# An encoder layer on one core: two gate products run along with the arrival of x, and two numbers of its planner are changed

## The chip, the core and the metric

The kernel runs on one core of a Trainium2 chip. The metric is the device time of one execution in microseconds (us), taken as the median over runs. Engines are named as in the profile: PE multiplies matrices (PEld loads its weights), DVE and ACT work elementwise, POOL and SP mostly issue transfers (DMA).

## The reference, cut to what matters

One layer over 512 tokens of 1024 channels, all in float32:

```
qa, ka, va, qb, kb, vb = split(x @ w_in)           # then partial rotary on q and k
o_a = windowed attention with sinks (16 query heads, 4 key heads)
o_b = three dilated window attentions (12 heads), merged
g_a, g_b = split(sigmoid(x @ w_gate + b_gate))     # w_gate: 1024 x 2048
y = (g_a * (o_a @ w_br_a) + g_b * (o_b @ w_br_b)) @ w_out
h = layer_norm(alpha * x + y)
out = layer_norm(alpha * h + (silu(h @ w_ff_gate) * (h @ w_ff_up)) @ w_ff_down)
```

## The kernel before, in words

**Numbers.** Each float32 operand is split into a high part `h` (a rounded copy) and a low part `l` (the rest). A product over 128 rows of the contraction is then three matmuls of 128 x 512: h by h, h by l, l by h. They stand on L513, L514 and L515 in `feat_k`, and one such call is called a product step here; a whole product over 1024 channels has eight (k = 0 to 7). A weight unit is 128 x 1024 values (512 KB), loaded in two halves of 256 KB. `half_unit` does it in the ordinary case: a transfer (L371, on SP's queue), a copy to `h` (L363, on ACT), a subtraction to `l` (L389, on DVE).

**The start.** The first units of k, q and v (`psk`, `psq`, `psv`, three PSUM banks) are multiplied while x arrives: x comes in eight blocks of 256 KB (xs[0] to xs[7], L481), each split by an L363 copy and an L486 subtraction, and PE takes k, q and v of block 0, then of block 1, and so on. The weights of these three are cut into pieces (`half_unit_by`, `CUTS`, subtractions on L422), and the table `FIRST` gives each piece its place among the transfers. Beside this, DVE and ACT form sums of the x blocks for later (`x_forms`, L534 and L560). Then an order written as a string (`ORDER`) goes on: `g2` two gate products (16 products of 128 columns make all gates), `VA` the second half of v and its transposes (L895), `q1` the next queries, `A0` the first attention group (scores on L860 and L861), and so on. `P:` products and all feed-forward products use seven half-size products for eight, for which some weights are sums of two blocks. Such a sum is fetched by `load_sum`: a plain transfer from SP, then one from POOL that adds while it writes (L377), an accumulating transfer.

**The branches.** After the attentions, `branch_a` and `branch_b` multiply their outputs by w_br_a and w_br_b; `gated` (L1387, on DVE) multiplies the gate with the bank and so makes it free, L1409 adds the two branches, L1355 (ACT) and L1363 (DVE) split the sum, and w_out is multiplied token-major (L1453 to L1455). At that time the first feed-forward weights are fetched already.

**The feed-forward** runs over 22 units of 128 columns (`quad`, matmuls on L1663 to L1665), with the down product in three chunks (`Chunk.step`, L1874 to L1876) between them and the rest token-major at the end. `silus` lists the activations of the units.

**What sets the order.** All operations are handed to a planner (`Program.run`), which goes through a clock of its own (`now`), starts on each engine the ready operation of the lowest priority number for which there are buffers, and issues it at once: the order in which it starts operations is the order of the instructions on each engine. It reckons an accumulating transfer's end thus (`moves` is the time of its bytes):

```
moved = max(moved, end + 0.3) + (1.0 if now < SLOW else 0.92) * o.moves
o.done = moved + (0.87 if e == ACT else 3.2 if now < SLOW else 2.2)
```

`SLOW` (300) is also the time after which plain transfers from SP are reckoned with an end 0.87 after their bytes, and not 2.4. Buffers are counted by class: `whl` (split weights), `ws` (weights as they land), `gen` (all else); `pr.spare` (12) is how many `gen` buffers are kept back from operations that are not first in line. `POOL 0.0` operations change such limits in the course of the plan.

Of the kernel before, what the change touches and what calls it, by code (L numbers as in the profile page):

```python
# [9 lines left out]
F32 = mybir.dt.float32  # L10
# [5 lines left out]
P = 128  # L16
S = 512
# [14 lines left out]
U_KA = 0  # L32
# [26 lines left out]
SPARE_OUT = 4  # L59
BANKS = dict(dense=3, s=2, tb=2, o=1, d=8)  # L60
UNITS = 2
SLOW = 300
SPIN = 4

CUTS = ((0, 128), (128, 256), (256, 512))
# [1 line left out]
         ("k", 1): (-996.9,), ("q", 1): (-996.7,), ("v", 1): (-996.6,),  # L67
         "x": (-999, -998.75, -997.5, -996.95, -996.8, -996.5, -996.4, -996.3)}
X_PACE = {1: None}
N_WS, N_WHL, N_ATT, N_GEN = 6, 12, 16, 60  # L70


# [5 lines left out]


ORDER = """  # L80
g2 VA q1 A0 q2 q3 g X k1 q4 A1 P:q5,g P:q6,q7 R A2 P:g,g A3 g g2 L Q00 K00 R Q01 K01 R V12 Q02 K02 R V0 B0 Q10 K10 R Q11 K11 R B1 Q12 K12 R B2 B3 g7
"""
FORMS = -60.0
PACK = -60.0
# [39 lines left out]
class Program:  # L124
# [67 lines left out]
    def run(self):  # L192
# [26 lines left out]
        while n_left:  # L219
# [11 lines left out]
            while progress:  # L231
                progress = False
                for e in engines:
# [27 lines left out]
                    if e == SP:  # L261
                        end = now + (0.62 if 14 < now < SLOW else 0.47)
                        moved = max(moved, now + 0.9) + (1.5 if now < 9.5 else 1.0 if now < SLOW else 0.92) * cost
                        o.done = moved + (2.4 if 14 < now < SLOW else 0.87)
                    elif o.moves:
                        end = now + cost
                        moved = max(moved, end + 0.3) + (1.0 if now < SLOW else 0.92) * o.moves
                        o.done = moved + (0.87 if e == ACT else 3.2 if now < SLOW else 2.2)
                    else:
                        end = now + cost  # L270
                        o.done = end
# [50 lines left out]
def hybrid_layer(ctx: ExitStack, tc: tile.TileContext, wpack, xT, xtok, sink, bgate,  # L322
# [6 lines left out]

    N_SLOT, HP = 85, S // 2  # L330
    pr = Program({"slot": N_SLOT, "bank": 8, **BANKS,
                  "ws": N_WSA, "whl": N_WHLA, "att": N_ATT, "gen": N_GEN,
                  "unit": UNITS, "st": 4, "x4": 4, "wf": N_WF})
    op = pr.op
    mm = nc.tensor.matmul
# [130 lines left out]

    first = {}
    for j in range(2):
        for w, u in (("k", U_KA), ("q", U_QA), ("v", U_VA)):
            first[w, j] = half_unit_by(u, j, ((0, S),) if j else CUTS, FIRST[w, j])  # L470
    got, xs = {}, []
    for j in range(KD):
        st, ap = slot(F32, "xs"), FIRST["x"][j]
# [751 lines left out]
        op([(SP, 0.73)], lambda e: nc.sync.dma_start(d.t, t.t), reads=[t], writes=[d], prio=EV)  # L1225
        away[f] = d

    def gate(f, put=False):
        ps = bank("dense")
        feat_x(ps, unit(U_GATE + f))  # L1230
        t = slot()
        gz[f] = t
        op([(ACT, act(S, True, 1))], lambda e: nc.scalar.activation(
            halves(t.t), back(ps.t), AF.Tanh, bias=bg.t[:, f:f + 1], scale=0.5),
           reads=[ps, bg], writes=[t], prio=EV)
        if put:
            d = Buf("dram", None, lambda: dram.tile([P, S], F32, name=name("gz")))
            op([(SP, 0.73)], lambda e: nc.sync.dma_start(d.t, t.t), reads=[t], writes=[d], prio=EV)
            away[f] = d

    def dense_q(u, nt, kv_half):
        ps = bank("dense")
# [6 lines left out]
        return k_post(ps, nt) if nt else k_pairs(ps)  # L1249

    psk, psq, psv = bank("dense"), bank("dense"), bank("dense")
    for k in range(KD):
        for w, ps in (("k", psk), ("q", psq), ("v", psv)):
            for c in (0, S // 2) if (w, k) == ("k", 0) else (None,):
                if c is None:
                    feat_k(ps, [first[w, 0], first[w, 1]], k, XM, xtok_of, split=w == "k")
                else:
                    op_ = feat_k(ps, [first[w, 0], first[w, 1]], k, XM, lambda k, c=c: [(xh4[0], 0, c), (xl4[0], 0, c)],
                                 n0=c, n1=c + S // 2, begins=c == 0, split=True)
                    if c == 0:  # L1260
                        fill(op_)
    ka = k_near(psk, 4)
    qa = q_near(psq, 4, (0, 0))
    load(mB, maskb, prio=0)
    env = {"gate": 0, "turn": [], "qs": {}, "ks": {}}

    def units_of(w):
        i = int(w[1:] or 0)
# [15 lines left out]
    def step(w):  # L1284
# [27 lines left out]
        elif w == "k1":  # L1312
            ka.extend(dense_k(U_KA + 1, 4))
        elif w[0] == "A":
            g = int(w[1])
            for b in range(NR):
                unit_a(g, b, qa[4 * g:4 * g + 4], ka[g], env["va"])
        elif w[0] in "gG":
            for _ in range(int(w[1:] or 1)):
                gate((env["gate"] + 8) % 16, w[0] == "G")  # L1320
                env["gate"] += 1
        elif w[0] in "QK":
            pair, g = int(w[1]), int(w[2])
            u, f = units_of(w)
            env["turn"].append((in_sbuf(u), f))
        elif w == "V0":
            env["v0"] = turned_values(U_V0, 8, 1)
        elif w == "V12":
            env["v1"], env["v2"] = token_values(U_VB)
        elif w[0] == "B":  # L1330
            hs = int(w[1])
            unit_b(hs, [env["qs"][hs // 2, g][hs % 2] for g in range(3)],
                   [env["ks"][hs // 2, g][hs % 2] for g in range(3)], env["v0"], env["v1"], env["v2"])
            if hs in ROOMS:
                op([(POOL, 0.0)], lambda e: pr.limits.update(ROOMS[hs]), after=list(exps))
# [575 lines left out]
            out[t, :, j * S + c0:j * S + c1], xt[t, j].t[:, c0:c1]), reads=[tok])  # L1911

    op([(POOL, 0.0)], lambda e: pr.limits.update(whl=4 * (N_LAST + 2)), after=[silus[-2]])
    n0 = 2 * N_PAIR * N_CHUNK
    tok_major(NFF - n0, N_LAST, lambda k: su[n0 + k], U_DOWN + n0, lg2, lb2, store, True, 1.0,
              lambda t: [chunks[c].step(n) for c, n in STEPS.get(("block", t), ())], (2, 3))
# [101 lines left out]
```

## Time and profile before

| | |
|---|---|
| median of 3 runs | 740.82 us (740.76 to 741.11) |
| the profiled execution | 739.78 us, of which the span of instructions is 737.9 us |
| busy | PE 723.1, PEld 662.9, DVE 661.0, ACT 460.7, POOL 118.8 us |
| granted PE clock | 0.998 |
| moved by DMA | 126.62 MB, on average 172 GB/s |

The profile is one execution, followed by the hardware. A row of its timeline is: start, duration, engine, line, operation, output and inputs, shapes, count, and in brackets the idle time before it with what ended that. Matmuls overlap in it: each is shown for 0.28 to 0.48 us, but one of 128 x 512 starts every 0.216 us when nothing holds PE. How long PE waits is therefore read from the starts.

### The profile page before, as it was taken

To read this page: it belongs to the slowest core of one execution; us is meant where nothing else is said; L and a number is where in the kernel's file an instruction comes from. 1 tells how busy PE (TensorE), PEld (TensorE's weight loads), DVE (VectorE), ACT (ScalarE), POOL (GpSimd) and SP (SyncE) were. 2 spreads that over 40 slices of the span, in tenths; PEclk is the share of its full clock that TensorE was granted. 3 is DMA by queue.
4 is the path that set the end of the run, shared out by engine and by line. 5 is a ranking of instruction groups with operands and counts; after the bars stand their busy time and mean duration, and the time that the engine had idled before them with its cause. 6 is when DMAs were issued, how large, how long until landed. Compare 5 with 4: busy or idle time off the path is not lost.

```text
span 737.9 us, 13854 instructions
## 1 busy us (share of the span) xinstructions
PE 723.1 (98%) x4587; PEld 662.9 (90%) x4587; DVE 661.0 (90%) x1445; ACT 460.7 (62%) x1041; POOL 118.8 (16%) x279
## 2 busy tenths in 40 slices
PE   8999999999999999999989999999999999999996
PEld 5888999888888888898878999999999999999985
DVE  6998999899888897789977999799999999899987
ACT  5765797776676676565643557656666556666721
POOL 0021001100000460360011012111102211212100
PEclk9999999999999999999999999999999999999999
DMA  8876666126724367745874289866888878978502
GB/s 261 268 178 164 159 197 170 41 84 160 202 66 122 121 182 194 197 138 169 267 191 115 74 251 229 191 176 153 203 247 200 223 183 234 250 198 176 118 29 85
DMA packets 73718, 126.62 MB, mean 172 GB/s; under 512 B 9904, under 2 KB 14128, under 8 KB 73648
## 3 DMA queue, kind: packets, MB, share of 16 engines
q1 hardware_dynamic: 62640, 105.96, 47.0%
q0 software_dynamic: 10736, 19.67, 16.5%
q8 instruction: 36, 0.59, 0.3%
q14 instruction: 34, 0.28, 0.1%
q10 hardware_dynamic: 272, 0.13, 0.1%
HBM read 106.32 MB, written 2.88 MB: 148 GB/s over the span
## 4 chain that ended last, share of the span: by engine, by line
PE 90%; DMA 5%; DVE 2%; SPq 1%; ACT 1%; issue 1%; DVEq 0%; ACTq 0%
PE ps L513 9%; PE ps L514 9%; PE ps L515 9%; PE ps L1663 9%; PE ps L1665 9%; PE ps L1664 9%; PE ps L1874 4%; PE ps L1876 4%; PE ps L1875 4%; PE ps L963 3%; PE ps L1453 3%; PE ps L1455 3%; PE ps L1454 3%; DMA sl<-wpack 2%; PE ps L861 1%; PE ps L860 1%
## 5 line engine op out<-in xcount | busy, mean ns | idle before, releaser
L363 ACT ACTIVATE sl<-sl 128x512 fp32r<-128x512 f32 (+3 forms) x401 | 220.9, 585 | 40.5 <-DVE sl L534 19.5
L534 DVE TENSOR_TENSOR sl<-sl,sl 128x512 fp32r<-128x512 f32 (+3 forms) x333 | 192.2, 615 | 8.0 <-DMA sl<-wpack 3.8
L363 ACT ACTIVATE sl<-ps 128x256 f32<-128x256 f32 (+6 forms) x210 | 89.9, 446 | 96.9 <-PE ps L1665 59.7
L513 PE MATMUL ps<-x,sl 128*128 128x512 f32 (+1 forms) x321 | 123.3, 384 | 0.9 <-ACT x L363 0.8
L515 PE MATMUL ps<-x,sl 128*128 128x512 f32 (+1 forms) x321 | 121.6, 379 | 0.4 <-DVE sl L422 0.4
L514 PE MATMUL ps<-x,sl 128*128 128x512 f32 (+1 forms) x289 | 109.8, 380 | 0.9 <-DVE x L486 0.8
L1663 PE MATMUL ps<-sl,sl 128*128 128x256 f32 x352 | 96.9, 275 | 0.6 <-ACT sl L363 0.6
L1664 PE MATMUL ps<-sl,sl 128*128 128x256 f32 x352 | 96.8, 275 | 0.0
L1665 PE MATMUL ps<-sl,sl 128*128 128x256 f32 x352 | 96.8, 275 | 0.0
L377 POOL DMA_DIRECT2D sl<-wpack x50 | 44.1, 886 | 314.0 <-DVE sl L534 95.2
L389 DVE TENSOR_TENSOR sl<-sl,sl 128x512 fp32r<-128x512 f32 x118 | 79.1, 684 | 3.5 <-ACT sl L363 3.1
L1663 PE MATMUL ps<-x,sl 128*128 128x256 f32 x264 | 72.6, 275 | 0.0
L1664 PE MATMUL ps<-x,sl 128*128 128x256 f32 x264 | 72.6, 275 | 0.0
L1665 PE MATMUL ps<-x,sl 128*128 128x256 f32 x264 | 72.6, 275 | 0.0
L515 PEld LDWEIGHTS ps<-x,sl 128*128 128x128 f32 x321 | 60.7, 189 | 9.4 <-DVE sl L422 0.9
L513 PEld LDWEIGHTS ps<-x,sl 128*128 128x128 f32 x321 | 60.8, 189 | 8.8 <-ACT x L363 1.5
L1663 PEld LDWEIGHTS ps<-sl,sl 128*128 128x128 f32 x352 | 67.6, 192 | 0.8 <-ACT sl L363 0.7
L1664 PEld LDWEIGHTS ps<-sl,sl 128*128 128x128 f32 x352 | 67.6, 192 | 0.1
L1665 PEld LDWEIGHTS ps<-sl,sl 128*128 128x128 f32 x352 | 67.6, 192 | 0.0
L514 PEld LDWEIGHTS ps<-x,sl 128*128 128x128 f32 x289 | 54.7, 189 | 8.2 <-DVE x L486 2.3
L1016 ACT ACTIVATE sl<-sl,st 128x257 f32<-128x257 f32 (+1 forms) x64 | 35.7, 560 | 26.9 <-DVE st L1012 25.0
L1663 PEld LDWEIGHTS ps<-x,sl 128*128 128x128 f32 x264 | 50.6, 192 | 0.4
(174 smaller groups left out, 1680.4 us busy)
## 6 DMA issues: line engine op xcount, KB each, us to landing
sl<-wpack SPq DMA_DIRECT2D x246, 256.0 KB, 3.9
sl<-sl SPq DMA_DIRECT2D x110, 128.0 KB, 2.4
wf<-wpack SPq DMA_DIRECT2D x51, 256.0 KB, 5.0
sl<-wpack POOLq DMA_DIRECT2D x50, 256.0 KB, 5.7
wf<-wpack POOLq DMA_DIRECT2D x24, 256.0 KB, 6.1
sl<-xtok SPq DMA_DIRECT2D x8, 256.0 KB, 4.0
sl<-sl SPq DMA_DIRECT2D x60, 32.0 KB, 2.0
out<-sl SPq DMA_DIRECT2D x7, 256.0 KB, 2.0
```

The costliest lines, as they stand in the source:

```text
L363: nc.scalar.activation(dst, src, AF.Copy)
L377: op([(POOL, 1.0)], lambda e: nc.gpsimd.dma_start(b.t, src2, accum_op=ALU.add), reads=[b], writes=[b], prio=prio, moves=1.65)
L389: op([(DVE, dve(S))], lambda e: nc.vector.tensor_tensor(l.t, src.t, f32(h.t), op=ALU.subtract), reads=[src, h], writes=[l], prio=prio, abs ...
L513: mm(o, a, x0, start=(k == 0 and begins), stop=False, skip_group_check=split)
L514: mm(o, a, x1, start=False, stop=False, skip_group_check=split)
L515: mm(o, b, x0, start=False, stop=(k == nk - 1), skip_group_check=split)
L534: op([(DVE, dve(w))], lambda e: nc.vector.tensor_tensor(dst(), x(), y(), op=o), reads=reads, writes=writes, prio=prio)
L1016: exps.append(op([(ACT, act(n + 1, extra=2))], lambda e, p=p, h=h: nc.scalar.activation(p.t[:, :n + 1], p.t[:, :n + 1], AF.Exp, bias=st.t[ ...
L1663: mm(o, wh, pairs(bh[k]()), start=(first and k == 0), stop=False, skip_group_check=True)
L1664: mm(o, wh, pairs(bl[k]()), start=False, stop=False, skip_group_check=True)
L1665: mm(o, wl, pairs(bh[k]()), start=False, stop=(k == 3), skip_group_check=True)
L1874: mm(ps.t, x0, pairs(w[0].t), start=(first and m == 0), stop=False, skip_group_check=True)
```

## The change

Three things are done.

1. The first two gate products (`N_ALONG = 2`, gates 8 and 9) move from the string (`g2`) into the start: they are multiplied with each x block just after k, q and v, into two banks of class `s`. Their weights are loaded with the start's (`half_unit_by`, first half in two pieces of 256 columns, `ALONG_CUTS`), at places that `FIRST` gives them: two pieces ahead of the last pieces of k, q and v's first halves, two behind, and the second halves among the later x blocks. The limit of `whl` begins at 24 and goes to 16 when the last of these product steps starts.
2. The planner reckons the end of an accumulating transfer as 6.2 behind its bytes while its clock stands between 330 and 420 (it was 3.2 or 2.2), and `SLOW` goes from 300 to 340.
3. From the third last activation of the feed-forward on, 8 `gen` buffers are kept back instead of 12.

```diff
-SLOW = 300
+SLOW = 340
+N_ALONG, N_WHL0 = 2, 24
+ALONG_CUTS = ((0, 256), (256, 512))
+FIRST.update({(0, 0): (-997.45, -996.97), (0, 1): (-996.65,), (1, 0): (-997.4, -996.96), (1, 1): (-996.45,)})
...
 ORDER = """
-g2 VA q1 A0 q2 q3 g X k1 q4 A1 P:q5,g P:q6,q7 R A2 P:g,g A3 g g2 L Q00 K00 ...
+VA q1 A0 q2 q3 g X k1 q4 A1 P:q5,g P:q6,q7 R A2 P:g,g A3 g g2 L Q00 K00 ...
...
-                        o.done = moved + (0.87 if e == ACT else 3.2 if now < SLOW else 2.2)
+                        o.done = moved + (0.87 if e == ACT else 6.2 if 330 < now < 420 else 3.2 if now < SLOW else 2.2)
...
-                  "ws": N_WSA, "whl": N_WHLA, "att": N_ATT, "gen": N_GEN,
+                  "ws": N_WSA, "whl": N_WHL0, "att": N_ATT, "gen": N_GEN,
...
-        for w, u in (("k", U_KA), ("q", U_QA), ("v", U_VA)):
-            first[w, j] = half_unit_by(u, j, ((0, S),) if j else CUTS, FIRST[w, j])
+        for w, u in (("k", U_KA), ("q", U_QA), ("v", U_VA), *((i, U_GATE + 8 + i) for i in range(N_ALONG))):
+            first[w, j] = half_unit_by(u, j, ((0, S),) if j else ALONG_CUTS if w in range(N_ALONG) else CUTS, FIRST[w, j])
...
-    def gate(f, put=False):
-        ps = bank("dense")
-        feat_x(ps, unit(U_GATE + f))
+    def gate(f, ps=None):
+        if ps is None:
+            ps = bank("dense")
+            feat_x(ps, unit(U_GATE + f))
...
     psk, psq, psv = bank("dense"), bank("dense"), bank("dense")
+    along = [bank("s") for _ in range(N_ALONG)]
     for k in range(KD):
-        for w, ps in (("k", psk), ("q", psq), ("v", psv)):
+        for w, ps in (("k", psk), ("q", psq), ("v", psv), *enumerate(along)):
...
+    op([(POOL, 0.0)], lambda e: pr.limits.update(whl=N_WHLA, ws=N_WSA), after=[pr.ops[-1]])
+    for f in range(N_ALONG):
+        gate(8 + f, ps=along[f])
...
-    env = {"gate": 0, "turn": [], "qs": {}, "ks": {}}
+    env = {"gate": N_ALONG, "turn": [], "qs": {}, "ks": {}}
...
     op([(POOL, 0.0)], lambda e: pr.limits.update(whl=4 * (N_LAST + 2)), after=[silus[-2]])
+    op([(POOL, 0.0)], lambda e: setattr(pr, 'spare', 8), after=[silus[-3]])
```

The matmuls are the same in number and shape before and after; what changes is where they stand. Lines after the change are 3 or 4 higher for the same statement (L513 is L516, L1387 is L1391).

On SP's queue at the start, after the third x block (`sl8`), before: the last pieces of k, q and v (`sl3`, `sl5`, `sl6`), then the fourth x block (`sl17`).

```order
L481 DMA sl8_98<-xT 128x512
L418 DMA sl3_75<-wpack 128x256
L418 DMA sl5_83<-wpack 128x256
L418 DMA sl6_85<-wpack 128x256
L481 DMA sl17_130<-xT 128x512
```

And after, where `sl12` and `sl13` are the two gates' first halves and `sl23` is the fourth x block:

```order
L484 DMA sl8_98<-xT 128x512
L421 DMA sl12_105<-wpack 128x256
L421 DMA sl13_109<-wpack 128x256
L421 DMA sl3_75<-wpack 128x256
L421 DMA sl5_83<-wpack 128x256
L421 DMA sl6_85<-wpack 128x256
L421 DMA sl12_105<-wpack 128x256
L421 DMA sl13_109<-wpack 128x256
L484 DMA sl23_159<-xT 128x512
```

Four pieces of 128 KB stand ahead of the fourth x block that did not, two of them ahead of the last pieces of k, q and v.

On PE at the same time, after block 1 of x, before: block 2 for k, q and v (`ps14`, `ps18`, `ps20`).

```order
L513 MATMUL ps14_112<-x47_94,sl9_100 128x512
L514 MATMUL ps14_112<-x411_103,sl9_100 128x512
L515 MATMUL ps14_112<-x47_94,sl10_101 128x512
L513 MATMUL ps18_134<-x47_94,sl12_109 128x512
L514 MATMUL ps18_134<-x411_103,sl12_109 128x512
L515 MATMUL ps18_134<-x47_94,sl13_110 128x512
```

And after: the two gates (`ps29`, `ps32`) for block 0, and then the same two for block 1.

```order
L516 MATMUL ps29_182<-x47_94,sl21_156 128x512
L517 MATMUL ps29_182<-x411_103,sl21_156 128x512
L518 MATMUL ps29_182<-x47_94,sl22_157 128x512
L516 MATMUL ps32_193<-x47_94,sl25_167 128x512
L517 MATMUL ps32_193<-x411_103,sl25_167 128x512
L518 MATMUL ps32_193<-x47_94,sl26_168 128x512
```

From block 2 on, all five follow each other for each block. What came after the two gate products before, comes directly after block 7 now.

On DVE in the branches, before: behind one L1387 stands the sum `sl1130`, which reads `sl1148`, a buffer that an accumulating transfer fills (L377); the next L1387 is two rows behind it.

```order
L1387 SCALAR_TENSOR_TENSOR sl379_1663<-sl379_1663,ps1176_5057 128x512
L534 TENSOR_TENSOR sl1130_4902<-sl1148_4963,sl1130_4902 128x512
L1409 TENSOR_TENSOR sl965_4166<-sl965_4166,sl379_1663 128x512
L1387 SCALAR_TENSOR_TENSOR sl1166_5024<-sl1166_5024,ps1170_5040 128x512
L1363 SCALAR_TENSOR_TENSOR sl1180_5086<-sl965_4166,sl1179_5085 128x512
```

And after:

```order
L1391 SCALAR_TENSOR_TENSOR sl374_1658<-sl374_1658,ps1176_5063 128x512
L1413 TENSOR_TENSOR sl965_4172<-sl965_4172,sl374_1658 128x512
L1367 SCALAR_TENSOR_TENSOR sl1180_5088<-sl965_4172,sl1179_5087 128x512
L1391 SCALAR_TENSOR_TENSOR sl1166_5030<-sl1166_5030,ps1170_5046 128x512
L1413 TENSOR_TENSOR sl945_4098<-sl945_4098,sl1166_5030 128x512
L537 TENSOR_TENSOR sl1182_5102<-sl1137_4936,sl1181_5101 128x512
L537 TENSOR_TENSOR sl1130_4908<-sl1148_4969,sl1130_4908 128x512
```

The sum that waits for the accumulating transfer has moved from one row behind the first L1387 to six rows behind it, past the second. PE's order of instructions is the same in both kernels from within the attention of mixer B (row 1313 of 4539) to row 4214, and again in the last 148 rows; between row 177 and row 1313, and between row 4214 and row 4391, it differs.

More of the change, by code (lines that the diff above doesn't have):

```diff
@@ L80 @@
 ORDER = """
-g2 VA q1 A0 q2 q3 g X k1 q4 A1 P:q5,g P:q6,q7 R A2 P:g,g A3 g g2 L Q00 K00 R Q01 K01 R V12 Q02 K02 R V0 B0 Q10 K10 R Q11 K11 R B1 Q12 K12 R B2 B3 g7
+VA q1 A0 q2 q3 g X k1 q4 A1 P:q5,g P:q6,q7 R A2 P:g,g A3 g g2 L Q00 K00 R Q01 K01 R V12 Q02 K02 R V0 B0 Q10 K10 R Q11 K11 R B1 Q12 K12 R B2 B3 g7
 """
@@ L1235, in gate @@
            reads=[ps, bg], writes=[t], prio=EV)
[L1236 to L1239, printed above, removed]
     def dense_q(u, nt, kv_half):
@@ L1319, in step @@
             for _ in range(int(w[1:] or 1)):
-                gate((env["gate"] + 8) % 16, w[0] == "G")
+                gate((env["gate"] + 8) % 16)
                 env["gate"] += 1
```

## The prediction

> **What bounds the kernel now.** I read the page's heads, then the stretches, then PE's timeline for every gap between starts.
>
> ```profile
> span 737.9 us, 13854 instructions
> PE 723.1 (98%) x4587; PEld 662.9 (90%) x4587; DVE 661.0 (90%) x1445; ACT 460.7 (62%) x1041; POOL 118.8 (16%) x279
> PE 90%; DMA 5%; DVE 2%; SPq 1%; ACT 1%; issue 1%; DVEq 0%; ACTq 0%
> ...
> core 0: us, PE busy (x) PEld busy (x) DVE busy (x) ACT busy (x) POOL busy (x), PEclk, DMA share, GB/s
> 0.00:10.00 10.00, 7.91 (x31) 4.82 (x32) 4.87 (x16) 4.82 (x12) 0.91 (x5) 1.00 0.69 183
> 10.00:20.00 10.00, 8.74 (x36) 5.92 (x35) 8.68 (x18) 6.99 (x13) 0.00 (x0) 1.00 1.01 342
> 20.00:30.00 10.00, 10.00 (x48) 8.77 (x47) 10.00 (x22) 6.83 (x14) 0.00 (x0) 1.00 0.93 301
> 30.00:45.00 15.00, 14.03 (x69) 12.00 (x68) 14.48 (x28) 11.73 (x22) 2.45 (x7) 1.00 0.82 244
> 45.00:380.00 335.00, 332.74 (x1887) 299.86 (x1884) 295.10 (x747) 223.07 (x537) 58.97 (x204) 1.00 0.56 156
> 380.00:400.00 20.00, 19.71 (x91) 17.15 (x92) 15.53 (x27) 9.39 (x16) 3.48 (x4) 1.00 0.55 136
> 680.00:700.00 20.00, 19.45 (x149) 18.54 (x148) 19.69 (x41) 16.00 (x38) 2.62 (x3) 1.00 0.61 138
> ```
>
> PE is busy for 98% of the span and carries 90% of the chain, at full clock in every stretch. The change takes no matmul away, so it can only win where PE waits: the first 20 us, the waits near 43 and 380 (in 45:380 PE lacks 2.26 of 335, which is the stretch from 377.74 to 380) and one near 688. These are the places, in PE's timeline:
>
> ```profile
> 10.14 0.38 PE L513 MATMUL ps<-x,sl 128*128 128x512 f32 x1
> ...
> 13.19 0.48 PE L514 MATMUL ps<-x,sl 128*128 128x512 f32 x1 [0.24 <-DVE x L486]
> ...
> 16.85 0.48 PE L515 MATMUL ps<-x,sl 128*128 128x512 f32 x1 [0.38 <-DVE sl L422]
> ...
> 18.73 0.48 PE L514 MATMUL ps<-x,sl 128*128 128x512 f32 x1 [0.53 <-DVE x L486]
> ...
> 24.44 0.38 PE L513 MATMUL ps<-x,sl 128*128 128x512 f32 x1
> ...
> 34.80 0.38 PE L513 MATMUL ps<-x,sl 128*128 128x512 f32 x1
> ...
> 43.17 0.55 PE L895 MATMUL ps<-ident,sl 128*128 128x128 f32 x3 [0.97 <-ACT sl L363]
> ...
> 47.23 0.27 PE L860 MATMUL ps<-sl,sl 128*128 128x256 f32 x1
> ...
> 377.36 0.38 PE L1455 MATMUL ps<-sl,sl 128*128 128x512 f32 x1
> 380.29 0.48 PE L513 MATMUL ps<-sl,sl 128*128 128x512 f32 x1 [2.55 <-DVE sl L1387]
> ...
> 687.83 0.28 PE L1665 MATMUL ps<-sl,sl 128*128 128x256 f32 x1
> 688.65 0.38 PE L1663 MATMUL ps<-sl,sl 128*128 128x256 f32 x1 [0.55 <-ACT sl L363]
> ```
>
> 10.14 is the first step of x block 2, 24.44 the first of the two gate products, 34.80 the first behind them. From 24.44 to 34.80 run 16 product steps without a gap: 10.36 / 16 = 0.6475 each. From 10.14 to 24.44 run 18 steps (six blocks of k, q, v), 11.65 of work in 14.30: **2.65 us are lost waiting for x and the weights.**
>
> **Part 1, the start.** Up to 10.14 PE's order is unchanged. After it stand 18 + 16 = 34 steps; with no wait they end at 10.14 + 34 x 0.6475 = 32.15 instead of 34.80. So the gain is 2.65 if the four new pieces and the x blocks arrive in time. Arrivals are read from ACT's copies:
>
> ```profile
> 8.21 0.40 ACT L363 ACTIVATE sl<-sl 128x256 fp32r<-128x256 f32 x1
> 9.87 0.42 ACT L363 ACTIVATE sl<-sl 128x256 fp32r<-128x256 f32 x1 [1.26 <-DMA sl<-wpack]
> 10.94 0.42 ACT L363 ACTIVATE sl<-sl 128x256 fp32r<-128x256 f32 x1 [0.65 <-DMA sl<-wpack]
> 11.78 0.63 ACT L363 ACTIVATE x<-sl 128x512 fp32r<-128x512 f32 x1 [0.42 <-DMA sl<-xT]
> ```
>
> These were k's, q's and v's last pieces and x block 3. The gates' first pieces now take the first two places (8.21, 9.87); copy and subtraction add some 0.8, so both are ready by 9.1 and 10.7, when PE wants them at 10.14 and 10.79. k, q, v and the gates' next pieces follow, and block 3 comes 512 KB later, at 342 GB/s 1.5 us: 13.3, ready by 14.6. PE does not ask for it before 10.14 + 9 x 0.6475 = 15.97. All start data end 1 MB later, 3.07 us at 342 GB/s, but PE's pace falls from 1.94 to 3.24 us per block, which covers that from block 4 on. Bounds: 2.65 gained; or all 3.07 shown as waiting, 0.4 lost. I take 2.3, nearer the first, because each arrival worked out lies ahead of its use.
>
> The extra splits also delay DVE, and k, q and v are complete later: block 7 of k ends at 10.14 + 30 x 0.6475 = 29.6; its rotation began at 23.70 before. What waits for them is the first transposes and scores.
>
> ```profile
> 14.11 0.42 DVE L534 TENSOR_TENSOR sl<-sl,sl 128x256 f32<-128x256 f32 x1
> 14.45 0.69 DVE L486 TENSOR_TENSOR x<-sl,x 128x512 fp32r<-128x512 f32 x1
> ...
> 23.70 0.68 DVE L731 TENSOR_TENSOR sl<-ps,sl 128x512 f32<-128x512 f32 x1
> 24.30 1.88 DVE L389 TENSOR_TENSOR sl<-sl,sl 128x512 fp32r<-128x512 f32 x3
> ```
>
> DVE takes 0.34 for 256 columns (14.11 to 14.45) and 0.60 for 512 (23.70 to 24.30). In its new order, 23 instructions of 512 and 11 of 256 stand from block 3's subtraction to the first rotation of k: 17.5 us from 13.8 on, to 31.3. Nothing is idle; it has done ahead what it did later before. From there 18 instructions lead to the first query part: 31.3 + 18 x 0.60 = 42.1. PE's new order puts v's second half, 8 steps of `q1` and 6 transposes ahead of the first score: 32.15 + 16 x 0.6475 + 0.66 = 43.2. The margin is 1 us. The transposes want ACT's copy of v's second half, which PE completes at 37.3; ACT's rows ahead of it wait for the rotation and split of k (nine DVE instructions, 36.7) and take some 1.8 with it: 38.5, against PE's 39.9. So the 0.97 at 43.17 goes too (0 to 0.97; I take it whole), and I allow 0.7 for a new wait in the reordered stretch up to B (0 to 3), since before it had none over 0.35 us there except the 0.97.
>
> **Part 2, the reckoned durations.**
>
> ```profile
> 373.89 0.69 DVE L1387 SCALAR_TENSOR_TENSOR sl<-sl,ps 128x512 f32<-128x512 f32 x1 [0.26 <-PE ps L515]
> 378.34 0.69 DVE L534 TENSOR_TENSOR sl<-sl,sl 128x512 f32<-128x512 f32 x1 [3.76 <-DMA sl<-wpack]
> 378.95 0.69 DVE L1409 TENSOR_TENSOR sl<-sl,sl 128x512 f32<-128x512 f32 x1
> 379.55 0.68 DVE L1387 SCALAR_TENSOR_TENSOR sl<-sl,ps 128x512 f32<-128x512 f32 x1
> ...
> 374.61 0.72 ACT L1462 ACTIVATE ps<-sl 128x512 f32<-128x512 f32 x1 [0.91 <-DVE sl L1387]
> ...
> 369.95 1.78 POOL L377 DMA_DIRECT2D sl<-wpack  x2 [42.28 <-PE ps L514]
> ```
>
> The accumulating transfer issued at 369.95 landed at 378.3, 8.3 us later. DVE stood 3.76 us before the sum that needs it; L1409 and the L1387 that frees PE's bank were queued behind, and PE waited 2.55. In the new order they go first: 373.89 + 0.60 = 374.5, L1409 to 375.1, L1363 behind ACT (whose 374.61 row ends at 375.3, then a copy of 0.63) to 376.6, L1387 to 377.2. PE asks at 377.36 + 0.22 = 377.58. The whole 2.55 goes; the sum, now next behind two instructions, would start at 378.4, as the bytes land, so DVE does not stand either. Late next is nothing that PE needs at once. Between 0 and 2.55 I take 2.4. `SLOW` moves no instruction of PE between rows 1313 and 4214: nothing.
>
> **Part 3, the buffers at the end.**
>
> ```profile
> 687.32 1.02 ACT L1851 ACTIVATE sl<-sl 128x256 fp32r<-128x256 f32 x3
> 688.24 0.64 ACT L363 ACTIVATE sl<-ps 128x256 f32<-128x256 f32 x2
> ```
>
> PE's wait at 688.65 is for a bank that ACT empties at 688.24, behind three L1851. With more buffers, chunk steps stand earlier and the L1851 apart from each other; that wait (0.55) may go or another of up to 1 may come, since DVE is busy 19.69 of 20 there. I take 0.3 gained.
>
> **Sum.** -2.3 - 0.97 + 0.7 - 2.4 - 0.3 = -5.3. The profiled execution took 739.78 (737.9 of span and 1.9 around it), 1.04 under the median; 734.5 there, **735.5 as a median.** About 0.2% (1.5 us) is what a measurement of this kernel can tell from no change.
>
> **The rivals.**
>
> *x comes late.* The DMA share is 1.01 in 10:20: the queues are full, and 1 MB more goes among the x blocks. If every byte delays x for PE, the start loses 0.4 instead of winning 2.3: 735.5 + 2.7 = 738.2. For it: the queue is full. Against it: PE needs a block only every 3.24 us. [...]
>
> *The wait moves only.* If the accumulating transfer lands later still, or ACT stands before a copy of the same weights, the wait near 380 stays: 735.5 + 2.4 = 737.9. For it: landing took 8.3 here, more than the 6.2 now reckoned. Against it: the rows in the new order.
>
> *Both*: 740.6, no change.
>
> *Late attention, slower.* From k's first rotation (23.70) to the first score (47.23) 23.5 us passed. If that chain took as long from 29.6 on, the score would be ready at 53.1 while PE comes to it at 43.2, and PE's order is fixed: 9.9 us of waiting, with nothing behind it allowed past. Then -2.65 - 0.97 + 9.9 - 2.55 = +3.7: 744.5. It decides from 6.2 us of waiting, a chain over 19.8. Against it: in the old chain DVE and ACT did weights and x sums between, which in the new order stand ahead of it. [...]
>
> **How the numbers follow.** Forecast 0.62; x late 0.12; the wait moves 0.12; both 0.07; late attention 0.07. Faster is the first three, 0.86; same 0.07; slower 0.07. The forecast's own range: all gains whole and no new wait, 740.82 - 2.65 - 0.97 - 2.55 - 0.55 = 734.1, with 0.7 for what is not seen 733.4; and with a new wait of 2 instead of 0.7, 736.8. The range reaches over the two faster rivals: 733.4 to 738.9.
>
> **What would show it.** Right: PE's steps follow each other from 10.1 to 32.2 without idle time; the first transposes and scores start by 43.5; no DVE wait for a transfer ahead of L1391 near 373, and PE's gap there under 0.3. Wrong: PE rows waiting for L489 or L425 between 10 and 32; a wait of over 2 us ahead of L898 or L863; a gap before an L516 in the branches; any wait over 1 us between 45 and 300.

## The result and the profile after

| | before | after |
|---|---|---|
| median | 740.97 us (740.43 to 741.79, 6 runs) | 734.34 us (733.43 to 735.17, 6 runs) |
| profiled execution | 739.78 us, span 737.9 | 734.55 us, span 732.7 |
| ratio after / before | | 0.991, 95% interval 0.9897 to 0.9923 |

The change makes the kernel faster: 6.63 us between the medians, 5.23 between the two profiled executions. That these two numbers differ is itself a finding; the experiments explain it.

The page of the changed kernel, its heads (span, busy time, chain that ended last):

```profile
span 732.7 us, 13850 instructions
PE 721.6 (98%) x4587; PEld 663.6 (91%) x4587; DVE 658.9 (90%) x1438; ACT 462.4 (63%) x1052; POOL 119.4 (16%) x279
PE 96%; DMA 2%; DVE 1%; SPq 0%; issue 0%; DVEq 0%; ACT 0%
```

PE is on 96% of the chain, against 90% before. The stretches of the changed kernel (bounds, length, busy time of each engine, granted clock, DMA share, GB/s):

```profile
core 0: us, PE busy (x) PEld busy (x) DVE busy (x) ACT busy (x) POOL busy (x), PEclk, DMA share, GB/s
0.00:10.00 10.00, 8.20 (x29) 4.81 (x30) 4.64 (x16) 5.42 (x13) 0.91 (x5) 1.00 0.69 197
10.00:20.00 10.00, 10.00 (x48) 8.74 (x47) 8.51 (x19) 7.35 (x16) 0.00 (x0) 1.00 0.99 335
30.00:45.00 15.00, 15.00 (x77) 13.17 (x76) 14.73 (x29) 11.53 (x23) 3.17 (x6) 1.00 0.81 233
45.00:370.00 325.00, 325.00 (x1849) 293.42 (x1848) 290.58 (x733) 222.74 (x542) 58.02 (x204) 1.00 0.55 156
370.00:390.00 20.00, 18.20 (x85) 15.53 (x84) 15.67 (x25) 10.28 (x17) 3.45 (x4) 1.00 0.86 206
680.00:700.00 20.00, 20.00 (x138) 18.79 (x138) 19.94 (x42) 15.27 (x34) 1.73 (x2) 1.00 0.26 57
```

PE is full in 10:20 (8.74 before), in 30:45 (14.03 before), in all of 45:370, and in 680:700 (19.45 before). Behind the first 10 us only 370:390 still has a hole: 18.20 of 20. It is one wait, in PE's timeline:

```profile
10.45 0.38 PE L516 MATMUL ps<-x,sl 128*128 128x512 f32 x1
...
32.47 0.38 PE L516 MATMUL ps<-x,sl 128*128 128x512 f32 x1
...
43.40 0.36 PE L863 MATMUL ps<-sl,sl 128*128 128x256 f32 x1
...
373.68 0.38 PE L1459 MATMUL ps<-sl,sl 128*128 128x512 f32 x1
375.86 0.48 PE L516 MATMUL ps<-sl,sl 128*128 128x512 f32 x1 [1.80 <-DVE sl L1391]
```

(The lines of the changed file stand three or four higher: L516 was L513, L863 L860, L1391 L1387, L1459 L1455, L1379 L1375.) 32.47 is the first step behind the products along with x, 43.40 the first score (47.23 before). The wait's cause is on DVE (first fence) and in SP's queue (second):

```profile
372.32 0.69 DVE L1367 SCALAR_TENSOR_TENSOR sl<-sl,sl 128x512 fp32r<-128x512 f32 x1 [0.70 <-ACT sl L1359]
375.11 0.69 DVE L1391 SCALAR_TENSOR_TENSOR sl<-sl,ps 128x512 f32<-128x512 f32 x1 [2.10 <-DMA sl<-gz]
```

```profile
363.76 0.86 SPq L374 DMA_DIRECT2D sl<-ln1g  x2
364.71 0.86 SPq L374 DMA_DIRECT2D sl<-ln1b  x2
365.66 0.38 SPq L374 DMA_DIRECT2D sl<-wpack  x1
366.13 0.40 SPq L1379 DMA_DIRECT2D sl<-gz  x1
```

and in the chain that ended last:

```profile
366.13 8.96 DMA sl<-gz
```

The sum of two weights no longer stands ahead of L1391. What L1391 waits for now is its other operand, the gate itself: it was put away in DRAM earlier and is fetched back (`fetch_gate`) behind four vectors of the layer norm and a weight half, and it takes 8.96 us to land.

From here, "gap" is the time between two starts on PE less what the first one takes when nothing holds PE (0.216 us for 128 x 512, half of that for 128 x 256, whose starts near 687 in before are 0.11 apart). By place, before and after:

| place | before | after | difference |
|---|---|---|---|
| 0 to 20 us, all gaps | 5.76 | 3.43 | -2.33 |
| near 43 | 1.2 | 0.0 | -1.2 |
| near 380 | 2.71 | 1.96 | -0.75 |
| 680 to 700, all gaps | 1.23 | 0.31 | -0.92 |
| sum | | | -5.2 |

The spans differ by 5.2, so these four places are all of it, to within 0.1.

### The profile page after: what moved, and what is told of

The parts are those of the page before. It is cut to its first block, busy times and chain, and to the rows that moved or that the text cites. A ratio compares the mean times of both kernels' runs of the same rounds, so it can differ in the third digit from the quotient of the medians.

```text
span 732.7 us, 13850 instructions
## 1 busy us (share of the span) xinstructions
PE 721.6 (98%) x4587; PEld 663.6 (91%) x4587; DVE 658.9 (90%) x1438; ACT 462.4 (63%) x1052; POOL 119.4 (16%) x279
## 4 chain that ended last, share of the span: by engine, by line
PE 96%; DMA 2%; DVE 1%; SPq 0%; issue 0%; DVEq 0%; ACT 0%
PE ps L516 11%; PE ps L517 11%; PE ps L518 11%; PE ps L1669 9%; PE ps L1667 9%; PE ps L1668 9%; PE ps L1878 4%; PE ps L1880 4%; PE ps L1879 4%; PE ps L966 3%; PE ps L1459 3%; PE ps L1458 3%; PE ps L1457 3%; PE ps L864 1%; PE ps L863 1%; PE ps L633 1%
## 5 line engine op out<-in xcount | busy, mean ns | idle before, releaser
L516 PE MATMUL ps<-x,sl 128*128 128x512 f32 (+1 forms) x321 | 123.8, 386 | 0.3 <-ACT x L366 0.3
L392 DVE TENSOR_TENSOR sl<-sl,sl 128x512 fp32r<-128x512 f32 x114 | 76.4, 685 | 6.0 <-ACT sl L366 5.7
L518 PEld LDWEIGHTS ps<-x,sl 128*128 128x128 f32 x321 | 60.7, 189 | 8.5
L516 PEld LDWEIGHTS ps<-x,sl 128*128 128x128 f32 x321 | 60.9, 190 | 7.6 <-ACT x L366 0.9
L517 PEld LDWEIGHTS ps<-x,sl 128*128 128x128 f32 x289 | 54.9, 190 | 6.6 <-DVE x L489 0.8
L1667 PEld LDWEIGHTS ps<-x,sl 128*128 128x128 f32 x264 | 50.6, 192 | 0.4
L1668 PEld LDWEIGHTS ps<-x,sl 128*128 128x128 f32 x264 | 50.6, 192 | 0.4
```

Source lines behind the costliest of these rows:

```text
L392: op([(DVE, dve(S))], lambda e: nc.vector.tensor_tensor(l.t, src.t, f32(h.t), op=ALU.subtract), reads=[src, h], writes=[l], prio=prio, abs ...
L516: mm(o, a, x0, start=(k == 0 and begins), stop=False, skip_group_check=split)
L517: mm(o, a, x1, start=False, stop=False, skip_group_check=split)
L518: mm(o, b, x0, start=False, stop=(k == nk - 1), skip_group_check=split)
L1667: mm(o, wh, pairs(bh[k]()), start=(first and k == 0), stop=False, skip_group_check=True)
L1668: mm(o, wh, pairs(bl[k]()), start=False, stop=False, skip_group_check=True)
```

## The experiments

Before's median is taken anew beside each set: 741.43 us (17 runs) for the three parts alone and the gate fetched early in the changed kernel, 741.38 (15) for the zeros in the wait, the gate fetched early in the kernel before, the gate fetched late and the gates ahead of x, 740.93 (11) for one gate along with x and both moves, 740.56 (9) for the zeros in the changed kernel.

**Part 1 alone.** The two gate products along with x, without the planner's numbers and the 8 buffers:

```diff
-SLOW = 340
+SLOW = 300
...
-                        o.done = moved + (0.87 if e == ACT else 6.2 if 330 < now < 420 else 3.2 if now < SLOW else 2.2)
+                        o.done = moved + (0.87 if e == ACT else 3.2 if now < SLOW else 2.2)
...
-    op([(POOL, 0.0)], lambda e: setattr(pr, 'spare', 8), after=[silus[-3]])
```

> The kernel before with the two gate products along with x, and nothing else of the change: PE's order is that of the changed kernel up to row 4214, and at the end that of the kernel before. Theory (each part acts in its own place): the start gains 2.3 us (PE's gaps from 0 to 20 us fall from 5.8 to 3.4) and the wait of 0.97 us near 43 goes; the wait near 380 of 2.5 us and the one near 688 of 0.55 us stay. About 3.5 us faster than before, 737.4. Rival (the start only shifts the whole, and the 1 us at 43 and at 688 were chance): 2.3 us faster or less. Rival (the earlier start also changes when transfers meet in the branches): the wait near 380 changes by more than 0.5 us.

Measured: 737.75 us (735.30 to 739.37, 6 runs), ratio 0.9951 (0.9934 to 0.9968). The gaps of 0 to 20 are 3.33, that near 43 is gone, that of 688 stays (0.72). So the whole start belongs to part 1. The wait near 377 is longer than before's, and what follows it is new, in PE's timeline:

```profile
376.95 0.48 PE L516 MATMUL ps<-sl,sl 128*128 128x512 f32 x1 [2.99 <-DVE sl L1391]
377.27 0.38 PE L517 MATMUL ps<-sl,sl 128*128 128x512 f32 x1
377.48 0.46 PE L518 MATMUL ps<-sl,sl 128*128 128x512 f32 x1
377.73 0.63 PE L516 MATMUL ps<-sl,sl 128*128 128x512 f32 x1
378.16 0.63 PE L517 MATMUL ps<-sl,sl 128*128 128x512 f32 x1
...
380.72 0.56 PE L1458 MATMUL ps<-sl,sl 128*128 128x512 f32 x1
381.11 0.38 PE L1459 MATMUL ps<-sl,sl 128*128 128x512 f32 x1
381.33 0.38 PE L1457 MATMUL ps<-sl,sl 128*128 128x512 f32 x1
```

From 377.73 to 381.1 the starts are 0.43 apart instead of 0.216: PE runs at half rate for 3.4 us, which costs 1.7. The six executions differ in the same way: two with a granted clock of 0.997 take 735.30 and 736.51 us, four with 0.993 to 0.995 take 737.66 to 739.37.

**Part 2 alone.** The kernel before with `SLOW = 340` and the 6.2:

```diff
-SLOW = 300
+SLOW = 340
...
-                        o.done = moved + (0.87 if e == ACT else 3.2 if now < SLOW else 2.2)
+                        o.done = moved + (0.87 if e == ACT else 6.2 if 330 < now < 420 else 3.2 if now < SLOW else 2.2)
```

> The kernel before with only the two reckoned durations changed (SLOW 340, and 6.2 for accumulating transfers between 330 and 420): PE's order is that of the kernel before in every row, and on DVE the sum that waits for an accumulating transfer stands behind the next L1387. Theory (the fetch of a gate from DRAM is the next late thing): the wait near 380 falls from 2.5 to some 1.8 us and is then put down to the gate's transfer in DVE's row: 0.7 us faster, 740.2. As the prediction had it (nothing else is late there): the wait goes whole, 2.5 us faster, 738.4.

Measured: 738.29 us (737.50 to 738.82, 5 runs), ratio 0.9964 (0.9952 to 0.9976). DVE's timeline shows the gate's fetch already here, and PE still waits 1.81 for it:

```profile
378.22 0.69 DVE L1387 SCALAR_TENSOR_TENSOR sl<-sl,ps 128x512 f32<-128x512 f32 x1 [2.11 <-DMA sl<-gz]
```

PE's gap is 1.97, only 0.74 shorter than in the profile of before, yet the median falls by 3.1. So the gap is what the theory of the gate's fetch said, and the time is what the other one said (738.4): the agreement of the time is luck, and the next runs show what else is in it.

**Part 3 alone.** The kernel before with the line on 8 buffers:

```diff
+    op([(POOL, 0.0)], lambda e: setattr(pr, 'spare', 8), after=[silus[-3]])
```

> The kernel before with only the 8 buffers kept back at the end instead of 12. Theory: the wait near 688 us (0.55 us before the row, 0.7 between starts) goes and nothing comes for it: 0.7 to 0.9 us faster, 740.1. Rival: that wait went in the changed kernel because everything upstream runs at another time, not by the buffers; then it is still there, and the time is that of before, 741.0.

Measured: 739.96 us (738.55 to 742.93, 12 runs), ratio 0.9989 (0.9975 to 1.0002). The wait at 688 is gone (680:700 below is full); the interval takes in no change, since the runs scatter. Up to the end PE's order is before's, so its profile shows what before can do near 380 in another execution, first by stretches (columns as above), then in PE's timeline:

```profile
376.00:380.00 4.00, 1.52 (x8) 0.98 (x6) 1.66 (x3) 0.33 (x1) 0.87 (x1) 1.00 1.06 217
380.00:384.00 4.00, 3.72 (x10) 3.03 (x11) 3.48 (x7) 2.52 (x6) 0.86 (x1) 0.57 0.43 73
680.00:700.00 20.00, 20.00 (x158) 19.36 (x157) 19.95 (x40) 15.14 (x35) 1.73 (x2) 1.00 0.57 125
```

```profile
377.14 0.38 PE L1455 MATMUL ps<-sl,sl 128*128 128x512 f32 x1
380.28 0.79 PE L513 MATMUL ps<-sl,sl 128*128 128x512 f32 x1 [2.76 <-DVE sl L1387]
380.87 0.63 PE L514 MATMUL ps<-sl,sl 128*128 128x512 f32 x1
381.30 0.63 PE L515 MATMUL ps<-sl,sl 128*128 128x512 f32 x1
...
383.43 0.47 PE L1454 MATMUL ps<-sl,sl 128*128 128x512 f32 x1
383.74 0.38 PE L1455 MATMUL ps<-sl,sl 128*128 128x512 f32 x1
```

After a wait of 2.76 the granted clock of the next 4 us is 0.57. The profile of before had a wait of 2.55 and 1.00 behind it (380:384). This suggests that the clock falls in part of before's executions too, and their granted clocks agree. The 52 executions of before that ran beside these experiments fall into two groups: 21 with a granted clock of 0.997 or 0.998 over the whole span take 738.81 to 740.38 us (median 739.82), 31 with 0.993 to 0.996 take 740.56 to 743.95 (median 741.59). The profiled execution (739.78, 0.998) is of the first group, the median of the second. Both groups occur in each of the four sets. Divided in the same way, part 3 alone gains about what was expected of it (0.7 to 0.9): its four executions with 0.997 or 0.998 have a median 1.1 under those of before beside them, its eight others 0.8 under the others.

**Zeros in the wait.** To test this, PE is kept busy without anything else being moved: in the kernel before, ten matmuls of zeros are added into the bank that is being accumulated, just ahead of the matmul that waits.

```diff
+                pr.n_kmm = getattr(pr, "n_kmm", 0) + 1
+                if pr.n_kmm == 9:
+                    for _ in range(10):
+                        mm(o, warm[:, :P], warm, start=False, stop=False, skip_group_check=True)
```

> The kernel before with ten matmuls of zeros (10 x 0.216 = 2.16 us), added into a bank that is being accumulated, queued on PE ahead of the matmul that waits near 380. They give nothing that is used and take none of the wait's cause away: the next product step still starts near 380.3. Theory (the idle time makes the clock fall in part of the executions, for some 3.4 us at half rate): with PE idle for under 0.9 us there the fall never comes, the median goes down by about 1 to 1.7 against before, to 739.7 to 740.4. Rival (the clock does not hang on the idle time): median as before's, or up by what of the 2.16 does not fit into the wait.

Measured: 740.00 us (739.45 to 740.65, 11 runs), ratio 0.9988 (0.9979 to 0.9997); the granted clock is 0.997 to 0.999 in all eleven. Its PE timeline:

```profile
376.79 0.38 PE L1455 MATMUL ps<-sl,sl 128*128 128x512 f32 x1
377.24 2.10 PE L1459 MATMUL ps<-warm 128*128 128x512 bf16 x9
379.96 0.48 PE L513 MATMUL ps<-sl,sl 128*128 128x512 f32 x1 [0.62 <-DVE sl L1387]
380.28 0.38 PE L514 MATMUL ps<-sl,sl 128*128 128x512 f32 x1
```

The useful step starts no sooner than its data allow, 2.16 us of useless work are added, and the median falls by 1.4, to that of before's first group. The second group is gone: by its granted clock none of eleven executions is in it, against ten of the fifteen of before beside them. So it was the idle time near 380 that made the clock fall; taken over to all 52 executions by their granted clock, it fell in 31. Three of these 31 (0.993, 743.09 to 743.95) are longer by some 2 us more, and no trace shows why. (The row counts nine of the ten; one record is missing.)

**Zeros in the wait of the changed kernel.** The control: seven matmuls of zeros at the same place in the changed kernel.

```diff
+                pr.n_kmm = getattr(pr, "n_kmm", 0) + 1
+                if pr.n_kmm == 9:
+                    for _ in range(7):
+                        mm(o, warm[:, :P], warm, start=False, stop=False, skip_group_check=True)
```

> The changed kernel with seven matmuls of zeros (7 x 0.216 = 1.51 us), whose result is used by nothing, queued on PE ahead of the matmul that waits 1.96 us near 376: the counterpart of the ten zeros in the kernel before. Theory (the change has already taken the idle time below what makes the clock fall, so there is nothing left to win by filling it): median 733.9 to 734.8, as the changed kernel's 734.3, granted clock as there. Rival (the zeros gain in some other way, so that what they gained in the kernel before is no proof of the clock): 733.3 or less.

Measured: 734.05 us (733.64 to 734.16, 5 runs), ratio 0.9912 (0.9895 to 0.9928), within 0.3 of the changed kernel. Zeros gain nothing where the idle time is 1.96: the change had already taken the clock's fall away (granted clock 0.996 to 0.999 in its six executions, 0.997 or 0.998 in these five).

**The gate fetched early.** In the changed kernel the gates' fetches get a place ahead of the vectors and weights:

```diff
-        op([(SP, 0.73)], lambda e: nc.sync.dma_start(t.t, d.t), reads=[d], writes=[t], after=after, prio=-20)
+        op([(SP, 0.73)], lambda e: nc.sync.dma_start(t.t, d.t), reads=[d], writes=[t], after=after, prio=-60)
```

> The changed kernel with the priority of the gates' fetches from DRAM at -60 instead of -20, so that the last of them is issued ahead of the vectors of the first norm and of seven weight loads; PE's order is that of the changed kernel in every row. Theory (the gap of 1.96 us at 375.9 is the wait for this fetch, which stood 9 us in full queues behind the vectors): the gap falls under 0.3 us, 1.7 us faster than the changed kernel, 732.6. Rival (the queues are full there, so another transfer of the same stretch, an accumulating one or a weight, is late in its place): a gap of 1 us or more stays within 15 us of it, and the time is within 0.7 us of the changed kernel's 734.3.

Measured: 732.03 us (731.96 to 732.23, 4 runs), ratio 0.9880 (0.9867 to 0.9893). The fetches go at 349.74, PE has no gap left there, the runs lie within 0.3 of each other. From SP's timeline, and the stretch:

```profile
349.74 1.71 SPq L1379 DMA_DIRECT2D sl<-gz  x2
```

```profile
370.00:390.00 20.00, 20.00 (x94) 17.53 (x93) 15.67 (x26) 9.49 (x16) 3.45 (x4) 1.00 0.88 217
```

So the fetch was what the change left over. That PE's order would be the changed kernel's in every row does not hold: since the gate is there, the planner puts the two product steps that waited (L516 at 375.86) ahead of six steps of w_out. The medians differ by 2.3 us, of which 1.96 is the gap, and the rest lies in the first 20 us, where executions of the same start differ by as much (3.1 to 3.4 in the experiments that leave the changed start alone). It is the fastest kernel of the study.

**The gate fetched early in the kernel before**, with the same edit and none of the change's parts:

> The kernel before with one number changed: the gates' fetches from DRAM go ahead of the layer norm's vectors and the next weights. None of the change's three parts is in. Theory (the wait near 380 is made by whichever transfer lands last there, and the clock falls after it in part of the executions): DVE's L1387 comes ahead of the sum, PE's wait of 2.9 goes, no matmul there runs at half pace; 2.7 of wait and about 1 on average for the clock: 737.3 to 738.2 (before: 741.4 in the last job). Rival (the accumulating transfer's reckoning is what counts, the gate's fetch follows by itself): the wait stays over 2 us and the median is within 0.7 of before.

Measured: 736.73 us (736.55 to 736.96, 5 runs), ratio 0.9940 (0.9925 to 0.9955), all at a clock of 0.997 or 0.998. In DVE's timeline L1387 is no longer behind a transfer:

```profile
374.02 0.69 DVE L1409 TENSOR_TENSOR sl<-sl,sl 128x512 f32<-128x512 f32 x1
374.62 1.28 DVE L1387 SCALAR_TENSOR_TENSOR sl<-sl,ps 128x512 f32<-128x512 f32 x2
```

One number brings 4.65 us at the median, more than part 2 (3.1): the gate comes early enough for the planner to put L1387 ahead of the sum by itself, whatever is reckoned for the sum, and on PE it moves the same two product steps as in the run before. My expectation was too careful by 0.6; I had counted the clock as 1 on average, and the median of before lies wholly in the second group, 1.77 above the first.

**The gate fetched late.** The gates' fetches of the changed kernel with a priority of -10. All three move behind vectors and weight loads, the last by 9.6 us (from 366.13 to 375.73), not by the 2 that were expected.

```diff
-        op([(SP, 0.73)], lambda e: nc.sync.dma_start(t.t, d.t), reads=[d], writes=[t], after=after, prio=-20)
+        op([(SP, 0.73)], lambda e: nc.sync.dma_start(t.t, d.t), reads=[d], writes=[t], after=after, prio=-10)
```

> The changed kernel with the last gate fetches put behind the layer norm's vectors and a weight load, some 2 us later. Theory: DVE's L1391 waits for gz that much longer; PE does two more steps of w_out ahead of it (1.3) and then waits about 2.7 to 3.5 us; matmuls behind the wait start 0.43 apart for 3 to 4 us in the profile, and the median is 1 + 1.7 above the changed kernel's: 736.4 to 737.4. Rival without the clock: no matmul at 0.43, median 735.0 to 735.6.

Measured: 734.46 us (733.61 to 735.56, 4 runs), ratio 0.9911 (0.9893 to 0.9928). Both expectations are missed. DVE and PE:

```profile
374.29 0.69 DVE L1391 SCALAR_TENSOR_TENSOR sl<-sl,ps 128x512 f32<-128x512 f32 x1 [5.61 <-DMA sl<-gz]
...
380.00 0.69 DVE L1391 SCALAR_TENSOR_TENSOR sl<-sl,ps 128x512 f32<-128x512 f32 x1 [1.17 <-DMA sl<-gz]
```

```profile
378.43 0.48 PE L1457 MATMUL ps<-sl,sl 128*128 128x512 f32 x1 [1.37 <-ACT ps L1466]
381.49 0.48 PE L1457 MATMUL ps<-sl,sl 128*128 128x512 f32 x1 [0.85 <-ACT ps L1466]
```

DVE stands 5.61 for the gate, but the planner has laid other steps of w_out ahead, and PE waits twice, 1.53 and 1.01 of gap, instead of once. Neither wait is as long as those behind which the clock fell (2.76 and 2.99), and it does not fall (from the second start on, those behind both waits are 0.21 to 0.22 apart again, and the granted clock of the execution is 0.998). So the run says nothing on a long wait; it adds that two short ones do no harm beyond their own length.

**The gates ahead of x.** All four first pieces of the two gates before the second pieces of k, q and v and the later x blocks:

```diff
-FIRST.update({(0, 0): (-997.45, -996.97), (0, 1): (-996.65,), (1, 0): (-997.4, -996.96), (1, 1): (-996.45,)})
+FIRST.update({(0, 0): (-998.6, -998.5), (0, 1): (-996.65,), (1, 0): (-998.55, -998.45), (1, 1): (-996.45,)})
```

> The changed kernel with all four first pieces of the two gates (512 KB) put ahead of the second pieces of k, q, v and of the later x blocks, which then come about 1.5 us later (512 KB at 342 GB/s). Theory (while PE has a product step for what has landed, the order of the pieces costs nothing): PE does the gates' steps of the first two blocks meanwhile (three steps, 1.94 us), the start loses what it loses in the changed kernel (3.4) to within 0.6, median 734.0 to 735.0. Rival (x late: bytes put ahead of x delay PE one for one): 1.5 more, 735.8.

Measured: 734.23 us (734.05 to 734.44, 4 runs), ratio 0.9907 (0.9891 to 0.9922). The gaps of 0 to 20 are 2.79; the changed start has 3.1 to 3.4 in five profiles. But PE's order is another up to about 60 us, and between 20 and 60 the gaps are 0.57 longer than in the changed kernel, 0.37 of it between two scores at 43. From 0 to 60 both lose the same to within 0.1. The 512 KB put ahead of x, 1.5 us at the 342 GB/s that before has in 10:20, cost PE nothing and gain nothing. (The wait for the gate near 374, untouched by the edit, is 1.38 in this profile.)

**One gate along with x.** `N_ALONG, N_WHL0 = 1, 20`, and the other gate product back in the string:

```diff
-N_ALONG, N_WHL0 = 2, 24
+N_ALONG, N_WHL0 = 1, 20
...
-VA q1 A0 q2 q3 g X k1 q4 A1 ...
+g VA q1 A0 q2 q3 g X k1 q4 A1 ...
```

> The changed kernel with one gate product along with the arrival of x instead of two (the other goes back behind it, as before). Theory (PE's work per x block against the pace of x): four steps are 2.59 us a block, against 1.94 without gates (2.65 us lost behind 10.1) and 3.24 with two (0.0 lost there); if x comes a block every 2.3 to 2.6 us at the full queues, one gate already covers all but 0 to 0.9: start loses 3.4 to 4.3, median 734.3 to 735.3. Rival (the gain grows with each gate alike): half of the 2.3 is lost, start 4.6, median 735.5.

Measured: 735.97 us (734.71 to 736.67, 6 runs), ratio 0.9932 (0.9910 to 0.9955). The profiled execution (734.97) has gaps of 3.65 in 0 to 20, against 3.43 with two gates: as the theory had it for the start, one gate already covers nearly all. The median is 0.7 above its bound. The profile shows two small waits that the changed kernel doesn't have (0.48 of gap at 289, and 0.32 at 19.3, which is in the 3.65), but a shorter one for the gate near 375 (0.89 against 1.96). What makes the other executions up to 1.7 longer than the profiled one is not seen in it; their granted clock is 0.997 or 0.998.

**Both moves.** The gates' pieces ahead of x and the early fetch together:

```diff
-FIRST.update({(0, 0): (-997.45, -996.97), (0, 1): (-996.65,), (1, 0): (-997.4, -996.96), (1, 1): (-996.45,)})
+FIRST.update({(0, 0): (-998.6, -998.5), (0, 1): (-996.65,), (1, 0): (-998.55, -998.45), (1, 1): (-996.45,)})
...
-        ... prio=-20)
+        ... prio=-60)
```

> The changed kernel with the gates' first pieces ahead (as in the run of that name) and the gates' fetches from DRAM ahead (as in the other). Theory: the two gains are at different places and add up: 732.0 - 0.6 = 731.4, start loses 2.8, no gap near 376. Rival (the order in between shifts and brings a wait of its own): 732.0 or over, with a gap over 0.3 somewhere between 30 and 370.

Measured: 734.09 us (733.60 to 734.55, 6 runs), ratio 0.9910 (0.9886 to 0.9935). The gains do not add. The start loses 2.64 and the gap near 376 is gone, but a small wait stands between two scores, as the rival said:

```profile
43.39 0.35 PE L863 MATMUL ps<-sl,sl 128*128 128x256 f32 x1 [0.20 <-DVE sl L764]
```

It is a gap of 0.37, and not new: the run with the gates ahead of x has the same one at 43.34, so that move had no gain that could add. Together, PE's gaps between 20 and 60 us are 0.8 longer than with the early fetch alone, more than the 0.43 won before 20, and PE's last matmul starts at 722.88 against 722.53. The rest of the difference between the spans (731.8 and 730.3) lies behind PE's end, 8.9 us against 7.8: the two 128 KB stores of `out` there take 2.6 us from issue to landing at the median in this execution, 2.0 in those of the early fetch alone and of the changed kernel. Why they do, and whether they do in the other five executions, is not known; the medians differ by 2.06, 0.65 more than these two spans.

## Why the prediction was right

The direction and the time hold: 735.5 was predicted in 733.4 to 738.9, and 734.34 was measured. Neither *x comes late* nor *late attention* came. *The wait moves only* came in its mechanism, though not in its time: of 2.71 us of gap near 380, 1.96 stayed, for a transfer that the rival didn't name. With it came one of the signs that I had named for being wrong, a gap before an L516 in the branches, and two for being right failed: DVE does wait for a transfer ahead of L1391 (2.10), and PE's gap there is not under 0.3. For the profiled execution I wrote 734.5, and it took 734.55. But that agreement is partly luck: two of the five terms held, three were off, and they cancel.

- **The start, -2.3: held, -2.33.** The steps follow each other without a gap from 10.45 to 32.47: 22.02 / 34 = 0.648 each. 0.3 was lost ahead of 10.45. Block 3's copy was worked out for 13.3 and k's first rotation for 31.3; the rows:

```profile
13.28 0.64 ACT L366 ACTIVATE x<-sl 128x512 fp32r<-128x512 f32 x1 [1.50 <-DMA sl<-xT]
...
31.89 0.69 DVE L734 TENSOR_TENSOR sl<-ps,sl 128x512 f32<-128x512 f32 x1
```

  *x comes late* fell: PE has no gap between 10.45 and 32.47, and the run with the gates ahead of x put 512 KB more ahead, without a loss to PE. The queues were full in the changed kernel too (the DMA share is 0.99 in 10:20). That does not decide who waits: PE asked for x later, for block 3 at 16.28, 3.0 after that block's copy began.
- **The wait at 43, -0.97: held.** The gap was 1.2 and is none. *Late attention* fell with it: the first score starts at 43.40 without a wait (43.2 predicted).
- **A new wait, +0.7: did not come.** PE is busy for 325.00 of 325 in 45:370.
- **The wait near 380, -2.4: the failing step.** I wrote "The whole 2.55 goes" and "Late next is nothing that PE needs at once". The gap lost 0.75. L1387 has three conditions: the bank, DVE's turn, and the gate; I cleared the first two and never asked for the third, because the row named only the last to come. Before's trace held it, in the tile view of the gate's fetch (issues, then the time from issue to landing):

```profile
L1375 SPq DMA_DIRECT2D sl<-gz x3: 326/382/1061, 346.9 to 369.8; - x3
...
DMA to landing us min/median/max: 2.1/4.0/7.7
```

  The last one is issued at 369.8. The landing times of this view are of six transfers, since it counts the three that put the gates away, too; the longest, 7.7, is that of the last fetch. It landed at 377.5, so my L1387 at 376.6 was not possible. In the changed kernel PE goes on 0.77 after the landing (375.09 to 375.86). With a landing at 377.51 that is 378.28, while PE asks at 377.58: 0.7 of gap would have stayed even so. The fetch then took 8.96 instead of 7.70, 1.26 more, and 0.70 + 1.26 is the 1.96 that was found. The run with the gate early in the changed kernel takes all of it away.
- **The end, -0.3: -0.92.** The wait at 688 went, and none came; part 3 alone does it.
- **The 1.04 between the profiled execution and the median.** I added it to 734.5 as if it were common to both kernels. It was not noise: it is the half rate that follows the wait near 380 in part of before's executions (31 of 52 by their granted clock, and none of the eleven with zeros in that wait). The change shortened that gap from 2.71 to 1.96, which is little, but it is enough to keep the clock: its six executions have 0.996 to 0.999 (the 0.996 is the second fastest of them), and the median lies with the profile. So part 2 was worth 0.75 in the gap and, at the median, the clock on top: 3.1 measured alone, against my 2.4. Of the 3.1, the gap's 0.74 and the 1.77 between before's two groups make 2.5; in its profile the first 20 us lose 0.58 less than in that of before, with the same instructions there, so the rest can be scatter of the start, which is not shown.

In short, 1.65 too much for the wait near 380, and 0.23, 0.7 and 0.62 too little for the wait at 43, the new wait and the end: these cancel to 0.1 in the profiled execution. Of the 1.16 between 735.5 and 734.34 the clock's 1.04 is nearly all.

The prediction read "at full clock in every stretch" from the one profile of before, with 1.00 behind a wait of 2.55. One execution was too little for that: by their granted clocks the fall came in 31 of 52 executions of the same kernel, and two traces show it, behind waits of 2.76 (part 3 alone, 0.57 in 380:384) and 2.99 (part 1 alone, starts 0.43 apart).

## What to carry to other kernels

When a wait is to be removed, list every operand and resource of the instruction behind it with the time at which each is there, the fetches above all; the row names only the last. Where a profiled execution is faster than the median by more than the spread, look at the granted clock of each execution: the difference may hang on one wait, and then shortening that wait a little is worth more than its length (part 2 alone: 0.74 off the gap, 3.1 off the median, of which 1.77 is what lies between before's two groups). Where PE's wait can't be removed, useless matmuls in it can pay: 1.4 us here in a wait behind which the clock fell, and nothing in one of 1.96.

## What the runs showed of the hardware

- The clock fell after single waits of 2.76 (part 3 alone) and 2.99 us (part 1 alone) and stayed after 1.80 (the changed kernel), 1.81 (part 2 alone), and in one execution of before 2.55. In the run of part 1 alone half rate lasted 3.4 us (starts 0.43 apart instead of 0.216), 1.7 us lost; the first matmuls behind the wait still ran at full rate (376.95 to 377.73), and the fall came 0.8 us later. In that of part 3 alone the starts from 380.87 to 383.43 are 0.43 apart.
- The fetch of a gate from DRAM (256 KB) took 4.4 to 9.0 us from issue to landing in the changed kernel, 8.96 for the last, which was issued behind four vectors and a weight half. Issued ahead of these (the last at 351.1), none of the three took over 5.2.
